# Hymba layer: the MLP's two products computed with seven of eight block products, up before down

## The chip, the cores and the metric

The kernel runs on one core of one Trainium2 chip. The metric is the device time of one execution in microseconds. Beside the runs without a profile there is one profiled execution, from which all views of the profile come.

## The reference

One decoder layer on x (1 x 1024 x 1024, float32): an attention part with two groups of heads, then the MLP that the change is about, then a last norm. Token count T = 1024, model width D = 1024, hidden width FF = 4096.

```python
def rmsnorm(x, g):
    xf = x.astype(jnp.float32)
    y = xf * lax.rsqrt(jnp.mean(jnp.square(xf), axis=-1, keepdims=True) + NORM_EPS)
    return (y * g.astype(jnp.float32)).astype(x.dtype)
...
    h = h + mix @ w_o
    v = rmsnorm(h, mlp_norm_g)
    h = h + jnp.square(jax.nn.relu(v @ w_up)) @ w_down
return rmsnorm(h, final_norm_g)
```

## The kernel before

Every float32 product is made of three TensorE products. A value is split into a high part (a cast to fp32r) and a low part (the value minus the high part), and a matmul group sums high x high, high x low and low x high. The high parts are casts on ScalarE or VectorE, the low parts subtractions on VectorE or POOL.

After attention `wo_ml(t)` (L1022) finishes the residual h for 128 tokens at a time, stores it to DRAM (`h_dram`) and normalises it; `v_tr(t)` (L1036) transposes the result on TensorE (8 transposes, L1042) into `vT`, the moving operand of the up product. The MLP runs in 16 chunks of 256 hidden columns. For each chunk:

- `w_split` (L1049) loads raw weights and splits them: high part on VectorE (L1053), low part on POOL (L1054).
- `up` makes four PSUM groups of 24 matmuls (L1076; 128x128 weights, 512 tokens). `up_act` squares the relu: ScalarE reads the bank (L1083), VectorE squares (L1084), ScalarE casts (L1085), POOL makes the low part (L1086).
- `down` (L1119) makes sixteen groups of 6 matmuls (L1131), and VectorE adds each to the residual in SBUF, `hacc` (L1133).

The order of TensorE is the order of the code (a manual schedule); a scheduler orders the other engines and SP's DMA queue. The main loop (end of the function) alternates: up of chunk c + 1, then down of chunk c; the last two chunks' down products are done together, 12 matmuls a group, and `finish_half` (L1137) norms and stores each 128 tokens behind them. `hacc` is loaded from `h_dram` (L1156) while the first chunk's up product runs. Half of that first product (th = 0) is placed between the last transposes. TensorE's MLP work is 16 x 96 up matmuls and 16 x 96 down matmuls.

Of the kernel before, what the change touches and what calls it, by code (L numbers as in the profile page):

```python
# [23 lines left out]
def tile_hymba_block(  # L24
# [1032 lines left out]
    def w_up_chunk(c):
        return [w_split(w_up[u * 512:(u + 1) * 512, c * FC * P:(c + 1) * FC * P].rearrange("(k p) f -> p k f", p=P),
                        [4, FC * P], s8) for u in range(2)]

    def w_down_chunk(c):
        return [w_split(w_down[(c * FC + u) * P:(c * FC + u + 1) * P, :], [D], wd_tile) for u in range(FC)]

    for t in range(NT):
        wo_ml(t)
        if t >= 2:
            v_tr(t - 2)
        if t == NT - 3:
            wu0 = w_up_chunk(0)
    def up_mm(wu, u, th):  # L1070
        tsl = slice(th * 512, (th + 1) * 512)
        ps = up_ps.tile([P, 512], F32, name="up", tag="up")
        n = 0
        for k in range(ND):
            for a, b in ((0, 0), (0, 1), (1, 0)):
                nc.tensor.matmul(ps[:], wu[k // 4][:, a, k % 4, u * P:(u + 1) * P], vT[:, b, k, tsl],  # L1076
                                 start=(n == 0), stop=(n == 3 * ND - 1))
                n += 1
        return ps

    def up_act(ps, hl, th, r):
        tsl = slice(th * 512, (th + 1) * 512)
        nc.scalar.activation(r[:], ps[:], AF.Relu)  # L1083
        nc.vector.tensor_mul(r[:], r[:], r[:])  # L1084
        nc.scalar.copy(hl[:, 0, tsl], r[:])  # L1085
        nc.gpsimd.tensor_sub(hl[:, 1, tsl], r[:], f(hl[:, 0, tsl]))  # L1086

    def up(c, wu):
        hid = []
        for u in range(FC):  # L1090
            hid.append(s8([P, 2, T]))
        for th in range(2):
            for u in range(FC):
                up_act(up_mm(wu, u, th), hid[u], th, relu_tile())
        return hid

    h0 = [s8([P, 2, T]) for _ in range(FC)]
    for u in range(FC):
        up_act(up_mm(wu0, u, 0), h0[u], 0,
               hp_pool.tile([P, D], F32, name="junk", tag="junk", bufs=3)[:, :512])  # L1100
        v_tr(NT - 2 + u)
# [4 lines left out]
    dn_ps = ctx.enter_context(tc.tile_pool(name="dn_ps", bufs=5, space=PSUM, reuse_waits="tile"))  # L1106
    mp_pool = ctx.enter_context(tc.tile_pool(name="mp_pool", bufs=1, reuse_waits="tile"))
    hacc = mp_pool.tile([P, NT, D], F32, name="hacc")
    gfb = mp_pool.tile([P, D], F32, name="gfb")
    def wd_tile(shape):  # L1110
        return mp_pool.tile(shape, F32R, name="wd", tag="wd", bufs=4)

    def relu_tile():
        return mp_pool.tile([P, 512], F32, name="rl", tag="rl", bufs=2)

    for u in range(FC):
        up_act(up_mm(wu0, u, 1), h0[u], 1, relu_tile())

    def down(cs, hid):  # L1119
        wd = [w for c in cs for w in w_down_chunk(c)]  # L1120
        nk = len(wd)
        final = cs[-1] == NCH - 1
        for t in range(NT):
            tsl = slice(t * P, (t + 1) * P)
# [85 lines left out]
```

## Time and profile before

| | |
|---|---|
| median of 3 runs | 1288.97 us (1288.13 to 1289.02) |
| profiled execution, span | 1286.3 us |
| PE (TensorE) busy | 1232.0 us, 96% |
| DVE (VectorE) busy | 721.8 us, 56% |
| POOL (GpSimd) busy | 480.7 us, 37% |
| ACT (ScalarE) busy | 401.1 us, 31% |
| read from HBM, written | 75.53 MB, 23.07 MB |

The profiled execution's own time stands here as its span: 2.7 us below the median of the other runs. Busy shares are averages over the whole span; the chain of waits and the timelines show which engine is waited for in a stage. Times in views are counted from the span's start.

### The profile page before, as it was taken

How to read it: one execution, taken by the hardware profiler on the slowest of the kernel's cores; microseconds unless marked ns; L12 is line 12 of the kernel's file. 1: busy time of each engine (PE TensorE's matmuls, PEld its weight loads, DVE VectorE, ACT ScalarE, POOL GpSimd, SP SyncE). 2: the span in 40 equal slices, each digit the busy share in tenths (PEclk: the TensorE clock that was granted, in tenths of full speed). 3: DMA queues.
4: the chain of work that ended last, by engine and by line, in shares of the span. 5: the costliest groups of instructions: out<-in, count | busy, mean ns of one | idle time of the engine just before them, and what ended most of it. 6: DMA issues, size and time to landing. Idle time of an engine off the chain costs nothing.

```text
span 1286.3 us, 15538 instructions
## 1 busy us (share of the span) xinstructions
PE 1232.0 (96%) x5808; PEld 1006.7 (78%) x5808; DVE 721.8 (56%) x1120; ACT 401.1 (31%) x916; POOL 480.7 (37%) x445
## 2 busy tenths in 40 slices
PE   9998988888799999999999999999999999999997
PEld 8877766666578888888888888888888888888886
DVE  8685589999997854564433443344334334433424
ACT  6433466666667831232011001101100110011022
POOL 3433444555634532216434224323432342243221
PEclk9999999999999999999999999999999999999999
DMA  6416635244511244644211112101201121021002
GB/s 214 123 58 204 157 74 123 58 103 105 186 58 50 88 160 146 222 156 162 72 59 56 43 33 66 49 33 50 66 34 47 52 61 38 33 67 49 1 33 98
DMA packets 64874, 112.17 MB, mean 87 GB/s; under 512 B 6304, under 2 KB 40608, under 8 KB 64288
## 3 DMA queue, kind: packets, MB, share of 16 engines
q1 hardware_dynamic: 64800, 111.20, 28.2%
q8 instruction: 45, 0.74, 0.2%
q14 instruction: 29, 0.24, 0.1%
HBM read 75.53 MB, written 23.07 MB: 77 GB/s over the span
## 4 chain that ended last, share of the span: by engine, by line
PE 69%; DVE 4%; ACT 1%; issue 1%; DMA 1%; POOL 0%; DVEq 0%; POOLq 0%; ACTq 0%; SPq 0%
PE dn L1131 28%; PE up L1076 27%; PE wo_p L962 3%; PE s L962 3%; DVE w L536 2%; PE mtr L828 1%; DMA kl<-klo 1%; PE s L740 1%; PE s L742 1%; PE s L741 1%; PE mav L845 1%; PE mav L846 1%; PE mav L847 1%; PE s L743 1%; PE s L744 1%
## 5 line engine op out<-in xcount | busy, mean ns | idle before, releaser
L1131 PE MATMUL dn<-wd,s 128*128 128x512 f32 x1536 | 360.7, 395 | 0.0
L1076 PE MATMUL up<-vT,s 128*128 128x512 f32 x1536 | 351.8, 389 | 0.6 <-DVE vT L693 0.4
L1131 PEld LDWEIGHTS dn<-wd,s 128*128 128x128 f32 x1536 | 288.3, 188 | 69.8
L1076 PEld LDWEIGHTS up<-vT,s 128*128 128x128 f32 x1536 | 288.1, 188 | 61.2 <-DVE vT L693 0.7
L1133 DVE TENSOR_TENSOR hacc<-hacc,dn 128x512 f32<-128x512 f32 x240 | 165.0, 688 | 147.1 <-PE dn L1131 147.0
L1054 POOL TENSOR_TENSOR wd<-raw,wd 128x1024 fp32r<-128x1024 f32 x32 | 82.1, 2565 | 321.8 <-DVE wd L1053 321.2
L1083 ACT ACTIVATE rl<-up 128x512 f32<-128x512 f32 x62 | 37.2, 599 | 516.5 <-PE up L1076 507.7
L1084 DVE TENSOR_TENSOR rl<-rl 128x512 f32<-128x512 f32 x62 | 47.8, 770 | 166.9 <-ACT rl L1083 166.9
L1086 POOL TENSOR_TENSOR s<-rl,s 128x512 fp32r<-128x512 f32 x62 | 80.7, 1302 | 87.7 <-ACT s L1085 87.7
L488 PE MATMUL mm<-xh,wt 128*128 128x512 f32 x256 | 87.9, 395 | 0.0
L549 PE MATMUL tr<-zid,b 128*128 128x128 f32 x288 | 52.6, 290 | 35.1 <-DVE al L557 25.5
L1054 POOL TENSOR_TENSOR s<-raw,s 128x1024 fp32r<-128x1024 f32 x32 | 77.6, 2427 | 21.6 <-DVE s L1053 12.8
L542 POOL TENSOR_TENSOR b<-b,w 128x512 f32<-128x512 f32 (+2 forms) x57 | 59.5, 1043 | 58.8 <-DVE w L536 39.5
L549 PEld LDWEIGHTS tr<-zid,b 128*128 128x128 f32 x288 | 33.0, 142 | 58.4 <-DVE al L557 44.2
L1053 DVE CAST wd<-raw 128x1024 fp32r<-128x1024 f32 x32 | 27.9, 872 | 76.2 <-DMA raw<-in_w_down_dram 76.1
L536 DVE TENSOR_TENSOR_SCAN w<-w,zid 128x129 f32<-128x129 f32 (+1 forms) x64 | 64.3, 1007 | 1.8 <-ACT w L531 1.6
L263 PE MATMUL acc<-wt,xh 128*128 128x448 f32 (+1 forms) x256 | 62.6, 378 | 1.4 <-ACT xh L214 1.4
L1085 ACT CAST s<-rl 128x512 fp32r<-128x512 f32 x62 | 38.6, 622 | 60.8 <-DVE rl L1084 60.8
L263 PEld LDWEIGHTS acc<-wt,xh 128*128 128x128 f32 x256 | 47.7, 188 | 8.9 <-ACT xh L214 2.0
L488 PEld LDWEIGHTS mm<-xh,wt 128*128 128x128 f32 x256 | 48.2, 189 | 8.3 <-issue 0.2
L488 PE MATMUL mm<-xl,wt 128*128 128x512 f32 x128 | 52.6, 411 | 0.0
L557 DVE TENSOR_TENSOR al<-tr,ah 128x512 fp32r<-128x512 f32 (+2 forms) x80 | 47.8, 597 | 5.8 <-ACT ah L556 5.4
(287 smaller groups left out, 1823.4 us busy)
## 6 DMA issues: line engine op xcount, KB each, us to landing
raw<-in_w_up_dram SPq DMA_DIRECT2D x32, 512.0 KB, 3.8
raw<-in_w_down_dram SPq DMA_DIRECT2D x32, 512.0 KB, 3.5
wr<-in_w_in_dram SPq DMA_DIRECT2D x24, 256.0 KB, 2.9
raw<-in_w_o_dram SPq DMA_DIRECT2D x8, 512.0 KB, 3.5
ht<-h_dram SPq DMA_DIRECT2D x8, 512.0 KB, 4.3
h_dram<-ht SPq DMA_DIRECT2D x8, 512.0 KB, 2.8
hacc<-h_dram SPq DMA_DIRECT2D x8, 512.0 KB, 7.6
xr<-in_xT_dram SPq DMA_DIRECT2D x14, 256.0 KB, 5.2
```

The lines of the kernel that those rows point to most:

```text
L263: nc.tensor.matmul(accs[t][:, :width], a[:, kk, t * P:(t + 1) * P], wts[kk][:, b, :width], start=(kk == 0 and p == 0), stop=done)
L488: nc.tensor.matmul(ps[:], wt[:, a, k % 4, :], b[:, k, tsl], start=(n == 0), stop=(n == 3 * ND - 1))
L536: nc.vector.tensor_tensor_scan(rv, rv, inject, init, ALU.mult, ALU.add)
L542: eng.tensor_mul(b[:, :n], b[:, :n], w[:, 1:n + 1])
L549: nc.tensor.transpose(tr[:, j * P:(j + 1) * P], sb_a[h, Q, C, j][:, s * P:(s + 1) * P], identf[:])
L557: nc.vector.tensor_sub(al[:, lo:], tr[:, lo:], f(ah[:, lo:]))
L962: nc.tensor.matmul(ps, hl[e][:, a, tsl], wt[e][:, b, dh * 512:(dh + 1) * 512], start=(n == 0), stop=(n == 11))
L1054: nc.gpsimd.tensor_sub(wt[:, 1], wr[:], f(wt[:, 0]))
L1076: nc.tensor.matmul(ps[:], wu[k // 4][:, a, k % 4, u * P:(u + 1) * P], vT[:, b, k, tsl], start=(n == 0), stop=(n == 3 * ND - 1))
L1086: nc.gpsimd.tensor_sub(hl[:, 1, tsl], r[:], f(hl[:, 0, tsl]))
L1131: nc.tensor.matmul(ps[:], hid[u][:, a, tsl], wd[u][:, b, dsl], start=(n == 0), stop=(n == 3 * nk - 1))
L1133: nc.vector.tensor_add(hacc[:, t, dsl], hacc[:, t, dsl], ps[:])
```

## The change

The up product hid = v x w_up is written as 2x2 blocks: per "quad" of 256 hidden columns the weights are four blocks A (each 512 of D by 128 columns), the transposed v four blocks B (512 of D by 512 tokens). Four blocks of the result come from seven block products in place of eight (the Winograd form): three use plain blocks of the weights, four use sums of blocks. A block product is 12 matmuls (`prod`).

- B11 and B21 are split straight out of the transposes of the first four token blocks, and their raw values go through DRAM (`r_dram`); R12 and R22 keep the raw values of the last four. The setup loop (`for j in range(4)`) makes the sums T1 to T4 and B22 out of them, each with its high and low part: per turn 5 casts on ScalarE, 6 operations on VectorE, 3 on POOL.
- For the first four quads, products 1 and 2 (which need B11 and B21 alone) are done ahead: `pre_quad(0)` and `(1)` between the last transposes, `(2)` and `(3)` behind the setup loop.
- `quad_w` makes the weight sums (4 VectorE operations) and splits seven weight blocks, low parts on POOL. `step` runs a product and adds on VectorE out of PSUM; `relu2` squares the relu. The sums of hidden values that down needs (s1 to s4) are made on VectorE, and all hidden values and sums go to DRAM: seven stores of 256 KB per quad.
- Down has the same form: seven chunks of 512 hidden columns, 7 products of 24 matmuls each, that collect in seven accumulators, four of which start from the residual (16 loads of 256 KB). Hidden values are loaded back (`ar`, 512 KB per product) and split: cast on ScalarE, low part on POOL. The last 512 hidden columns (two quads) are done plainly: 192 matmuls, 12 a group, with `finish_half` behind each.
- All of up is done before down begins. PSUM pools are renamed (3 + 5 banks for up, 8 for down); `raw_pool` has 2 buffers in place of 3.

The diff, cut to its core:

```diff
+    def split2(hi, lo, src, eng):
+        nc.scalar.copy(hi, src)
+        eng.tensor_sub(lo, src, f(hi))
+
+    def prod(ps, w, bv, start, stop):
+        n, last = 0, 3 * HD - 1
+        for k in range(HD):
+            for a, b in ((0, 0), (0, 1), (1, 0)):
+                nc.tensor.matmul(ps, w[:, a, k, :], bv[:, b, k, :], start=start and n == 0, stop=n == last,
+                                 skip_group_check=True)
+                n += 1
...
+    def pre_quad(q):
+        x = x_of[q]
+        ps = a_ps.tile([P, 512], F32, name="pa", tag="pa")
+        prod(ps[:], x[:, 0], B11, True, True)
+        p1 = o_tile("p1")
+        nc.scalar.copy(p1[:], ps[:])
+        prod(ps[:], x[:, 1], B21, False, True)
+        hid = o_tile("ho")
+        nc.scalar.activation(hid[:], ps[:], AF.Relu)
+        nc.vector.tensor_mul(hid[:], hid[:], hid[:])
+        p1_of[q] = (p1, hid)
+        store_hid(q, V_A11, hid[:])
...
+    pre_quad(0)
+    v_tr(NT - 2)
+    pre_quad(1)
+    pre_w(3)
+    v_tr(NT - 1)
...
+    nc.sync.dma_start(f(T1[:, 1]), r_dram[0][:])
+    nc.sync.dma_start(f(T4[:, 1]), r_dram[1][:])
+    for j in range(4):
+        c = slice(j * P, (j + 1) * P)
+        tt = s8([P, 4, HD, P], F32)
+        nc.vector.tensor_sub(tt[:, 0], R12[:, :, c], f(T1[:, 1, :, c]))
+        nc.vector.tensor_sub(tt[:, 1], R22[:, :, c], tt[:, 0])
+        nc.gpsimd.tensor_sub(tt[:, 2], R22[:, :, c], R12[:, :, c])
+        nc.vector.tensor_sub(tt[:, 3], f(T4[:, 1, :, c]), tt[:, 1])
+        for n_, (bv, sv) in enumerate(((T2, tt[:, 1]), (T1, tt[:, 0]), (T3, tt[:, 2]), (B22, R22[:, :, c]), (T4, tt[:, 3]))):
+            split2(bv[:, 0, :, c], bv[:, 1, :, c], sv, nc.gpsimd if n_ in (2, 3) else nc.vector)
...
+    pre_quad(2)
+    pre_quad(3)
...
+        split2(a22[:, 0], a22[:, 1], r22, nc.gpsimd)
+        w[V_A22] = a22[:]
+        nc.vector.tensor_add(r22, r21, r22)
+        nc.vector.tensor_sub(r21, r11, r21)
+        nc.vector.tensor_sub(r11, r22, r11)
+        nc.vector.tensor_sub(r12, r12, r11)
...
+        for tl, v, key, r_ in ((y, 0, V_S2, r11), (y, 1, V_S1, r22), (z, 0, V_S3, r21), (z, 1, V_S4, r12)):
+            split2(tl[:, v, 0], tl[:, v, 1], r_, nc.gpsimd)
...
+            elif what == 2:
+                prod(s_["a"][:], w[V_A12], B21, False, True)
+                s_["c11"] = o2_tile("ho")
+                nc.scalar.activation(s_["c11"][:], s_["a"][:], AF.Relu)
+                nc.gpsimd.tensor_mul(s_["c11"][:], s_["c11"][:], s_["c11"][:])
+                store_hid(q, V_A11, s_["c11"][:])
+            elif what == 6:
+                prod(bank("b"), w[V_S2], T2, True, True)
+                s_["u2"] = o_tile("u2")
+                nc.vector.tensor_add(s_["u2"][:], s_["b"][:], s_["p1"][:])
...
+        order = (1, 2, 6, 5, 7, 3, 4) if pair else (6, 5, 7, 3, 4) if pre else (1, 6, 5, 7, 2, 3, 4)
...
+    for q in range(NQ - 2):
+        quads([q], q < NPRE)
+    quads([NQ - 2, NQ - 1])
...
+    nc.sync.dma_start(gfb[:], gfin.to_broadcast([P, D]))
+    for q in range(4):
+        nc.sync.dma_start(acc[2][:, q], h_dram[q][:, 0:512])
+        nc.sync.dma_start(acc[3][:, q], h_dram[q][:, 512:])
+        nc.sync.dma_start(acc[4][:, q], h_dram[q + 4][:, 0:512])
+        nc.sync.dma_start(acc[7][:, q], h_dram[q + 4][:, 512:])
...
+        for i in (1, 2, 3, 5, 7, 6, 4):
+            ar = dn_pool.tile([P, 2, 512], F32, name="ar", tag="ar", bufs=4)
+            nc.sync.dma_start(ar[:], hv_dram[c][:, A_OF[i]])
+            av = s8([P, 2, 2, 512])
+            split2(av[:, 0], av[:, 1], ar[:], nc.gpsimd)
+            prep(i)
+            for q in range(4):
                 ps = dn_ps.tile([P, 512], F32, name="dn", tag="dn")
                 n = 0
-                for u in range(nk):
+                for u in range(2):
                     for a, b in ((0, 0), (0, 1), (1, 0)):
...
+                dst = acc[i][:, q]
+                if c == 0 and i in (1, 5, 6):
+                    nc.scalar.copy(dst, ps[:])
+                else:
+                    nc.vector.tensor_add(dst, dst, ps[:])
...
+    for u in range(4):
+        split2(lh[u][:, 0], lh[u][:, 1], hr[:, u], nc.gpsimd)
+        lb.append(s8([P, 2, D]))
+        split2(lb[u][:, 0], lb[u][:, 1], lw[:, u], nc.vector)
+    for q in range(4):
+        g = {i: acc[i][:, q] for i in acc}
+        nc.vector.tensor_add(g[2], g[2], g[1])
+        nc.vector.tensor_add(g[6], g[6], g[1])
+        nc.vector.tensor_add(g[5], g[5], g[6])
+        nc.vector.tensor_add(g[3], g[3], g[5])
+        nc.gpsimd.tensor_add(g[4], g[4], g[6])
+        nc.gpsimd.tensor_add(g[4], g[4], g[7])
+        nc.vector.tensor_add(g[7], g[7], g[5])
```

Three places of the order. First, VectorE where the MLP begins. Before (junk and rl are hidden values, s and wd split weights, vT the low parts of the transposes):

```order
L1033 SCALAR_TENSOR_TENSOR junk<-ht,nss,ssq_s 128x1024
L693 TENSOR_TENSOR vT<-vtr,vT 128x4x128
L1084 TENSOR_TENSOR junk<-junk 128x512
L693 TENSOR_TENSOR vT<-vtr,vT 128x4x128 x2
L1084 TENSOR_TENSOR junk<-junk 128x512
L693 TENSOR_TENSOR vT<-vtr,vT 128x4x128 x2
L1053 CAST s_6402<-raw 128x1024
L1053 CAST s_6407<-raw 128x1024
L1053 CAST wd<-raw 128x1024
L1084 TENSOR_TENSOR rl<-rl 128x512 x3
```

Now (ho are hidden values, r are R12 and R22, t the T tiles, s the loop's scratch tiles; L1076 are the low parts of `split2`):

```order
L1122 TENSOR_TENSOR ho<-ho 128x512 x2
L1151 TENSOR_TENSOR s_6389<-r_5836,t_6383 128x512
L1151 TENSOR_TENSOR s_6404<-r_5836,t_6383 128x512
L1152 TENSOR_TENSOR s_6389<-r_5837,s_6389 128x512
L1076 TENSOR_TENSOR t_6383<-s_6389,t_6383 128x4x128
L1152 TENSOR_TENSOR s_6404<-r_5837,s_6404 128x512
L1076 TENSOR_TENSOR t_6382<-s_6389,t_6382 128x4x128
L1076 TENSOR_TENSOR t_6383<-s_6404,t_6383 128x4x128
L1154 TENSOR_TENSOR s_6389<-t_6386,s_6389 128x512
L1154 TENSOR_TENSOR s_6404<-t_6386,s_6404 128x512
L1076 TENSOR_TENSOR t_6382<-s_6404,t_6382 128x4x128
```

The two squares of early hidden values stand ahead of the setup loop, and in place of a few splits VectorE has the loop's 24 operations, of which the first ten are shown; two more squares and the weight sums of the first quad follow them.

Second, SP's queue where the residual is loaded. Before, among the first up products (h_dram holds the residual):

```order
L1031 DMA h_dram_109<-ht 128x1024
L1031 DMA h_dram_110<-ht 128x1024
L1156 DMA hacc<-h_dram_103 128x1024
L1156 DMA hacc<-h_dram_104 128x1024
...
L1156 DMA hacc<-h_dram_110 128x1024
L1157 DMA gfb<-in_gfin_dram 128x1024
L1051 DMA raw<-in_w_down_dram 128x1024
L1051 DMA raw<-in_w_up_dram 128x4x256 x2
L1051 DMA raw<-in_w_down_dram 128x1024 x2
L1051 DMA raw<-in_w_up_dram 128x4x256 x2
```

Now, between up and down (the acc tiles are the accumulators, wr the weights of down, ar its hidden values):

```order
L1108 DMA hl_dram<-ho 128x512 x7
L1285 DMA gfb<-in_gfin_dram 128x1024
L1108 DMA hl_dram<-ho 128x512
L1287 DMA acc_8697<-h_dram_103 128x512
L1288 DMA acc_8698<-h_dram_103 128x512
L1289 DMA acc_8702<-h_dram_107 128x512
L1290 DMA acc_8700<-h_dram_107 128x512
...
L1290 DMA acc_8700<-h_dram_110 128x512
L1299 DMA wr<-in_w_down_dram 128x2x1024 x2
L1331 DMA ar<-hv_dram_5840 128x1024 x7
L1299 DMA wr<-in_w_down_dram 128x2x1024 x2
```

The loads of the residual have moved behind the last hidden store of up, and the first weights and hidden values of down stand behind them.

Third, POOL ahead of the last stage. Before (s are the hidden values' low parts, fss the sums of `finish_half`):

```order
L1054 TENSOR_TENSOR s_10187<-raw,s_10187 128x1024
L1086 TENSOR_TENSOR s_9921<-rl,s_9921 128x512
L1054 TENSOR_TENSOR wd<-raw,wd 128x1024 x2
L1086 TENSOR_TENSOR s_10190<-rl,s_10190 128x512
L1086 TENSOR_TENSOR s_10191<-rl,s_10191 128x512
L1086 TENSOR_TENSOR s_10190<-rl,s_10190 128x512
L1086 TENSOR_TENSOR s_10191<-rl,s_10191 128x512
L1143 TENSOR_TENSOR fss<-fss 128x1
L82 TENSOR_SCALAR rs_mean<-fss 128x1
L83 TENSOR_TENSOR fss<-rs_mean,mhalf 128x1
```

Now (acc_8702 is accumulator 4, lh the split hidden values of the last two quads; L1372 and L1373 are the loop's two POOL sums):

```order
L1076 TENSOR_TENSOR s_10705<-ar,s_10705 128x1024
L1076 TENSOR_TENSOR s_10709<-wr,s_10709 128x1024
L1372 TENSOR_TENSOR acc_8702<-acc_8702,acc_8701 128x512
L1373 TENSOR_TENSOR acc_8702<-acc_8702,acc_8700 128x512
L1372 TENSOR_TENSOR acc_8702<-acc_8702,acc_8701 128x512
L1373 TENSOR_TENSOR acc_8702<-acc_8702,acc_8700 128x512
L1076 TENSOR_TENSOR lh_10748<-hr,lh_10748 128x1024
L1076 TENSOR_TENSOR lh_10749<-hr,lh_10749 128x1024
L1076 TENSOR_TENSOR lh_10752<-hr,lh_10752 128x1024
L1076 TENSOR_TENSOR lh_10753<-hr,lh_10753 128x1024
L1372 TENSOR_TENSOR acc_8702<-acc_8702,acc_8701 128x512
L1373 TENSOR_TENSOR acc_8702<-acc_8702,acc_8700 128x512
L1372 TENSOR_TENSOR acc_8702<-acc_8702,acc_8701 128x512
```

The four low parts of the plain rest stand behind four sums of accumulator 4, where before the low parts of the last chunk were the only work.

## Rows read from the trace of the kernel before

**Rows 1.** the page's head and its first part: busy time, share of the span, instructions

```profile
span 1286.3 us, 15538 instructions
...
PE 1232.0 (96%) x5808; PEld 1006.7 (78%) x5808; DVE 721.8 (56%) x1120; ACT 401.1 (31%) x916; POOL 480.7 (37%) x445
```

**Rows 2.** the page's chain that ended last, by line: shares of the span

```profile
PE dn L1131 28%; PE up L1076 27%; PE wo_p L962 3%; PE s L962 3%; DVE w L536 2%; PE mtr L828 1%; DMA kl<-klo 1%; PE s L740 1%; PE s L742 1%; PE s L741 1%; PE mav L845 1%; PE mav L846 1%; PE mav L847 1%; PE s L743 1%; PE s L744 1%
```

**Rows 3.** the chain in order of time, MLP: start us, length us, engine and line

```profile
569.38 5.49 PE up L1076 x24
574.87 0.87 PE vtr L1042 x8
...
638.33 21.77 PE up L1076 x96
660.11 22.39 PE dn L1131 x96
...
1234.27 44.81 PE dn L1131 x192
```

**Rows 4.** groups of equal shape on VectorE, ScalarE, POOL: busy us, mean ns | idle before

```profile
L1133 DVE TENSOR_TENSOR hacc<-hacc,dn 128x512 f32<-128x512 f32 x240 | 165.0, 688 | 147.1 <-PE dn L1131 147.0
...
L1030 DVE SCALAR_TENSOR_TENSOR ht<-wo_p,rs_mla,ht 128x512 f32<-128x512 f32 x16 | 11.7, 744 | 5.1 <-PE wo_p L962 5.1
...
L1033 DVE SCALAR_TENSOR_TENSOR junk<-ht,nss,ssq_s 128x1024 f32<-128x1024 f32 x8 | 10.3, 1284 | 7.6 <-POOL nss L83 7.6
...
L1085 ACT CAST s<-rl 128x512 fp32r<-128x512 f32 x62 | 38.6, 622 | 60.8 <-DVE rl L1084 60.8
...
L1017 ACT ACTIVATE junk<-ht 128x1024 f32<-128x1024 f32 x8 | 8.5, 1062 | 10.6 <-DVE ht L1030 10.6
...
L1086 POOL TENSOR_TENSOR s<-rl,s 128x512 fp32r<-128x512 f32 x62 | 80.7, 1302 | 87.7 <-ACT s L1085 87.7
L1054 POOL TENSOR_TENSOR s<-raw,s 128x1024 fp32r<-128x1024 f32 x32 | 77.6, 2427 | 21.6 <-DVE s L1053 12.8 <-POOL s L1086 8.8
```

**Rows 5.** timeline of TensorE, 581 to 584 us: start, length, instructions, [idle before]

```profile
582.38 0.49 PE L1076 MATMUL up<-vT,s 128*128 128x512 f32 x1 [0.29 <-ACT vT L692]
583.23 0.96 PE L1076 MATMUL up<-vT,s 128*128 128x512 f32 x3 [0.36 <-DVE vT L693]
```

**Rows 6.** timelines of VectorE and of POOL, 583 to 602 us

```profile
585.79 2.89 DVE L1053 CAST wd<-raw 128x1024 fp32r<-128x1024 f32 x1
589.41 2.07 DVE L1084 TENSOR_TENSOR rl<-rl 128x512 f32<-128x512 f32 x1 [0.73 <-ACT rl L1083]
...
600.35 0.69 DVE L1084 TENSOR_TENSOR rl<-rl 128x512 f32<-128x512 f32 x1 [4.80 <-ACT rl L1083]
...
585.40 5.54 POOL L1054 TENSOR_TENSOR s<-raw,s 128x1024 fp32r<-128x1024 f32 x2 [0.68 <-DVE s L1053]
...
601.78 1.29 POOL L1086 TENSOR_TENSOR s<-rl,s 128x512 fp32r<-128x512 f32 x1 [4.20 <-ACT s L1085]
```

**Rows 7.** windows (busy us of five engines, PEclk, DMA share, GB/s), and a DMA issue

```profile
10.00:15.00 5.00, 5.00 (x27) 4.63 (x26) 5.00 (x9) 4.65 (x8) 1.04 (x1) 1.00 0.98 355
...
580.00:585.00 5.00, 4.35 (x23) 3.26 (x22) 3.12 (x4) 2.08 (x4) 1.31 (x1) 1.00 1.03 418
...
raw<-in_w_down_dram SPq DMA_DIRECT2D x32, 512.0 KB, 3.5
```

**Rows 8.** two windows at half the clock, and an instruction just before the first

```profile
98.69 0.55 PE L392 MATMUL tr<-zid,ce 128*128 128x128 f32 x3 [3.10 <-DVE rstd_b L453]
...
99.70:103.00 3.30, 3.30 (x14) 2.70 (x12) 1.50 (x2) 1.06 (x2) 0.00 (x0) 0.50 0.61 225
...
311.40:314.60 3.20, 3.20 (x14) 2.94 (x13) 3.20 (x7) 2.96 (x8) 2.79 (x3) 0.50 0.76 168
```

**Rows 9.** timelines of VectorE and of POOL, 616 to 623 us

```profile
618.38 1.27 DVE L1133 TENSOR_TENSOR hacc<-hacc,dn 128x512 f32<-128x512 f32 x2
...
617.87 1.74 POOL L1086 TENSOR_TENSOR s<-rl,s 128x512 fp32r<-128x512 f32 x1
```

More of the change, by code (lines that the diff above doesn't have):

```diff
@@ L1057, in w_up_chunk @@
[L1057 to L1062, printed above, removed]
+            if t < 4:
+                bb = (B11, B21)[dq]
+                split_out(tr[:], bb[:, 0, :, c], bb[:, 1, :, c])
+                stg = vraw_pool.tile([P, HD, P], F32, name="stg", tag="stg", bufs=3)
+                nc.scalar.copy(stg[:], tr[:])
+                nc.sync.dma_start(r_dram[dq][:, :, c], stg[:])
+            else:
+                nc.scalar.copy((R12, R22)[dq][:, :, c], tr[:])
@@ L1068, in tile_hymba_block @@
         if t == NT - 3:
[L1069 to L1101, printed above, removed]
+            for q in range(3):
+                pre_w(q)
+    pre_quad(0)
[3 more added lines that the diff above has]
+    v_tr(NT - 1)
     wo_stack.close()
@@ L1105, in tile_hymba_block @@
     rope_stack.close()
[L1106 to L1124, printed above, removed]
-            for dh in range(2):
-                dsl = halves[dh]
+    bcd_ps = mlp_psum.enter_context(tc.tile_pool(name="bcd_ps", bufs=5, space=PSUM, reuse_waits="tile"))
+    vb_stack = ExitStack()
+    vb_pool = vb_stack.enter_context(tc.tile_pool(name="vb_pool", bufs=1, reuse_waits="tile"))
@@ L1134, in down @@
-                if final:
-                    finish_half(t, dh)
-    def finish_half(t, dh):
+                dst = acc[i][:, q]
+                if c == 0 and i in (1, 5, 6):
+                    nc.scalar.copy(dst, ps[:])
+                else:
+                    nc.vector.tensor_add(dst, dst, ps[:])
+    for c in range(NQ // 2 - 1):
+        down(c)
+    dn_stack.close()
+    ld_pool = ctx.enter_context(tc.tile_pool(name="ld_pool", bufs=1, reuse_waits="tile"))
+    lh = [ld_pool.tile([P, 2, T], F32R, name=f"lh{u}") for u in range(2)]
@@ L1138, in finish_half @@
+    for q in range(4):
+        g = {i: acc[i][:, q] for i in acc}
[6 more added lines that the diff above has]
+        nc.vector.tensor_add(g[7], g[7], g[5])
+    fin = {}
+    def finish_half(t, dh, hx):
         if dh == 0:
-            fin.append((mp_pool.tile([P, 4], F32, name="fss", tag="fss", bufs=3), s8([P, D], F32)))
```

222 lines of the change are left out of this document (191 added, 31 removed).

## The prediction

> **What bounds the kernel now.** I read the head of the page first: TensorE is busy for 1232.0 of the 1286.3 us [rows 1]. Then the chain by line: the down and up products hold 28% and 27% of the span [rows 2]. The chain in order of time shows how: from 569.38 it is product after product, 96 up matmuls in 21.77 us and 96 down matmuls in 22.39, with one hand-over between [rows 3]. So the MLP is TensorE's own time, and other engines count only where TensorE is made to wait. One up matmul costs 21.77 / 96 = 0.2268 us, one down matmul 0.2332. The MLP's whole matmul time is 16 x 21.77 + 14 x 22.39 + 44.81 = 706.6 us.
>
> The profiled execution lasts 1286.3 us, 2.7 below the median of the runs shown (1288.97). The sum is made against 1286.3, and 2.7 is added at the end. A difference under 0.2%, 2.6 us, can't be told from none.
>
> **What goes.** Up now has 16 quads x 7 products x 12 = 1344 matmuls, down 7 chunks x 7 x 24 + 192 = 1368, so 360 of 3072 are gone. The shape stays (a 128x128 weight tile, 512 columns), so I take each product's own row: 1344 x 0.2268 + 1368 x 0.2332 = 304.8 + 319.0 = 623.8, **82.8 us less**. If the new tiles of up run at down's 0.2332 it is 74.2; if down runs at up's rate it is 91.5.
>
> **What comes, 1: the start of up.** TensorE is at 569.38 when its up products begin, in both kernels. Ahead of the first product that needs T2 stand four early pairs of products (96 x 0.2268 = 21.8) and two blocks of transposes (2 x 0.87 [rows 3]). The second product of a pair adds to the bank from which ScalarE copies the first, so it waits for a copy (0.62 by a cast of the same size [rows 4]) and a hand-over (about 0.36 [rows 5]): 1.0 each. The last transposes so end at 569.4 + 11.0 + 1.7 + 2.0 = 584.1. Then R12 and R22 are copied out (0.6 each, to 585.3) and the setup loop makes T1 to T4 and B22: 24 VectorE operations, each with both inputs in SBUF, and 12 on POOL. Such an operation takes 0.69 on VectorE (600.35, with POOL idle until 601.78 [rows 6]) and 1.30 on POOL [rows 4].
>
> Do the two run side by side? In rows 6, VectorE's operation at 589.41 took 2.07 us in place of 0.69 and ended just after the POOL pair that ran from 585.40; the cast at 585.79 took 2.89, and that POOL pair 5.54 in place of 2 x 2.4. An operation that meets the other engine's waits for it. I take them one after the other: 24 x 0.69 + 12 x 1.30 = 32.2, so 617.5. Behind them VectorE has two squares and three weight combinations for S2 (3.5), then come ScalarE's cast (0.62) and a low part on POOL (1.30): T2 and S2 are there at 622.9. TensorE has work for 23.5 of the 53.5 us from 569.4, so it idles 30, against 1 us in the same place before (0.29 + 0.36 and their hand-overs [rows 5]): **+29**. If the loop's two engines overlapped in full, VectorE's 16.6 us alone would set it, the product would start near 607.3, and the term is +13; if eight hand-overs of 0.36 between the engines are added it is +32. The Trainium skill (SBUF — State Buffer, "Who interferes with whom") says that a VectorE instruction with two SBUF inputs and a GpSimd instruction that reads SBUF share a port pair, and the later one blocks fully. By that rule the term is +29, by engines that run freely +13; rows 6 side with the rule.
>
> **2: between up and down.** Before, up and down products alternated, and the residual was loaded under running products. Now down can't start until all of up is through, and SP issues in order: the last hidden store, 16 loads of 256 KB into the accumulators, the first 2 MB of down weights, then the first 512 KB of hidden values. Let up's last matmul end at U. The last store waits for an addition and a square (0.69 + 0.74 [rows 4], with hand-overs U + 1.75). Behind it 4.2 MB go at 355 to 418 GB/s [rows 7], say 11 us, the weights take 5.0 and the values 1.25 at 418. A single 512 KB load lands 3.5 us after its issue [rows 7], 2.2 more than its bytes need: U + 21.2. ScalarE's cast (1.06) and POOL's low part (2.43) follow [rows 4]: U + 24.7. Nothing of TensorE's lies in between: **+25**, between +21 (no latency, all at 418) and +29 (all at 355, the latency once for the weights and once for the values). The same chain stands before the second and third products of the first chunk, whose low parts come from the same POOL: **+2.5** (0 to 5).
>
> **3: the last 512 rows.** POOL's order is two pairs of accumulator sums, then the four low parts of the last hidden rows. The sums wait for the last Strassen product's evictions. Let that product end at E. Its first group is evicted at about E - 3.5; four sums of 1.30 bring POOL to E + 1.7, and four low parts of 2.43 to E + 11.4. The first output group needs all four: its last three matmuls (0.7) end at E + 12.1 in place of E + 2.8, so 9.3 us are lost, and VectorE's 1024-wide low parts (1.28 [rows 4]) push between POOL's. I take **+12**, between +8 (sums that start earlier) and +17 (POOL waits for each of VectorE's four).
>
> **4: the clock.** Twice in the kernel before, TensorE got a granted clock of 0.50, the level of 1.2 GHz: the first time just after it had been idle for 3.10 us; the windows at 0.50 are 3.30 and 3.20 us long, full of work [rows 8]. That costs 1.7 us each time. The changed kernel has three idle stretches longer than 3.10: **+5** (0 to 9).
>
> **5: work that should be hidden.** In up each full quad has 7 low parts and one square on POOL (8 x 1.30 = 10.4), and on VectorE 11 operations with both inputs in SBUF (8 x 0.69 + 3 x 0.74 = 7.7) and 5 additions from PSUM (3.4). TensorE takes 84 x 0.2268 = 19.05 per quad. 10.4 + 7.7 = 18.1 fits. The additions from PSUM do not wait for POOL: at 618.38 two took 1.27 together beside POOL's operations, as long as two alone [rows 9]. An early quad has 13.6 us of TensorE time against 5 x 1.30 + 7.7 = 14.2, a loss of 0.6 four times. In down each chunk has 10 POOL low parts (24.3), and 8 VectorE operations 1024 wide (10.2) beside 28 additions from PSUM (19.3); TensorE takes 39.2, so 34.5 of exclusive work fits with little to spare. On SP a quad's seven stores of 256 KB, each waiting for its square or sum, stand ahead of later quads' weight loads; a quad later is 19 us, so this costs nothing unless VectorE falls a quad behind. I take **+4** for both stages (0 to 45, the second rival).
>
> Sum: -82.8 + 29 + 25 + 2.5 + 12 + 5 + 4 = -5.3. Span 1281.0, and with 2.7 a time of **1283.7 us**. The seven-product saving is nearly eaten by two places at which TensorE stands still.
>
> **The rivals.**
> *The setup runs side by side (faster).* The term of 29 becomes 13: 1283.7 - 16 = 1267.7. For it: POOL's twelve operations are 15.6 us in all, and those that fall where VectorE waits for one of ScalarE's 20 casts cost nothing. Against it: rows 6.
> *Blocking reaches the additions from PSUM (slower).* Then POOL's 10.4 and all of VectorE's 11.1 add up to 21.5 per full quad against 19.05, and 6.5 + 11.1 = 17.6 against 13.6 per early one: 12 x 2.4 + 4 x 4.0 = 45 in place of the 4 above, a time near 1325. It decides as soon as the two together exceed 19.05 per quad. For it: VectorE works its queue in order, so an addition stands behind a blocked operation, and TensorE waits for a bank. Against it: rows 9, and five banks that give slack.
> *The new tiles take the slow rate.* Up at 0.2332 gives 1344 x 0.0064 = 8.6 back: 1292.3. For it: two rates in one kernel for the same shape show that the operands, or where they lie, matter; against it: the shapes and the weights' side are those of up.
> *Every wait at its upper end.* +32, +29, +5, +17, +9 in place of 29, 25, 2.5, 12, 5 is 18.5 more: 1302.
> That the change doesn't remove the matmuls is excluded: they are counted in TensorE's order, 1344 and 1368.
>
> **How the numbers follow.** Forecast 0.32, its own range 1276 to 1291; setup side by side 0.22; slow rate 0.19; all waits long 0.15; blocking 0.12. The forecast lies under the bound of 1286.4 for four fifths of its chance and within 0.2% for the rest; the slow rate is half within, half above 1291.5. Faster 0.26 + 0.22 = 0.48; same 0.06 + 0.09 = 0.15; slower 0.10 + 0.15 + 0.12 = 0.37. The range runs from 1265, a little under the fast rival, to 1308, over the long waits, and leaves out the blocking rival and little else.
>
> **What would show it.** In the changed profile: 2712 MLP matmuls at 0.227 and 0.233; one idle stretch of TensorE of about 25 us that ends on POOL's or VectorE's last setup operation near 622; one of about 25 us before the first down product, which ends on POOL's low part behind the accumulator loads; one of 9 to 12 us before the last 192 matmuls; between these no TensorE idle time over 2 us per quad or chunk. The prediction is wrong if setup operations show 0.69 beside POOL's, if the boundary is under 15 us, or if TensorE waits inside the quads.

## The result and the profile after

The changed kernel takes 1297.2 us (median of 4 runs, 1295.69 to 1300.3) against 1288.96 before: 1.0062 times as long, 95% interval 1.0045 to 1.0079. It is slower by 0.6%. The sum said 5.3 us less; it is about 8 us more. The profiled execution's span is 1293.9 us, 7.6 over that of before.

The page of the changed kernel, its head, busy times and chain:

```profile
span 1293.9 us, 15840 instructions
...
PE 1167.7 (90%) x5448; PEld 946.9 (73%) x5448; DVE 946.3 (73%) x1300; ACT 531.2 (41%) x1078; POOL 643.9 (50%) x539
...
PE 24%; DVE 8%; POOL 7%; DMA 4%; issue 3%; ACT 1%; SPq 0%; DVEq 0%; POOLq 0%; ACTq 0%
```

TensorE did get 360 instructions less (5448 in place of 5808) and 64 us less busy time than in [rows 1]. But the chain that was nearly all TensorE in the MLP [rows 2, 3] now runs through VectorE, POOL and transfers as well. Where TensorE stands still is in its timeline; the main ones after an idle time of over half a microsecond are these, and the first two matmuls of the last stage (start, length, instructions, [idle before and releaser]):

```profile
572.03 3.02 PE L1082 MATMUL pa<-b,s 128*128 128x512 f32 x12 [0.68 <-ACT p L1118]
...
587.11 5.73 PE L1082 MATMUL pa<-b,s 128*128 128x512 f32 x24 [1.11 <-ACT p L1118]
599.12 5.30 PE L1082 MATMUL pa<-b,s 128*128 128x512 f32 x12 [6.28 <-ACT p L1118]
617.47 4.99 PE L1082 MATMUL pb<-t,s 128*128 128x512 f32 x12 [13.05 <-ACT s L1075]
672.27 4.59 PE L1082 MATMUL pd<-b,s 128*128 128x512 f32 x12 [1.92 <-DVE u L1223]
...
791.56 3.05 PE L1082 MATMUL pd<-b,s 128*128 128x512 f32 x12 [0.72 <-DVE u L1223]
...
812.08 3.06 PE L1082 MATMUL pd<-b,s 128*128 128x512 f32 x12 [0.78 <-DVE u L1223]
...
890.59 7.54 PE L1082 MATMUL pa<-b,s 128*128 128x512 f32 x24 [4.56 <-ACT p L1209]
950.92 0.80 PE L1340 MATMUL dn<-s,s 128*128 128x512 f32 x1 [24.79 <-ACT s L1075]
953.49 19.21 PE L1340 MATMUL dn<-s,s 128*128 128x512 f32 x72 [1.77 <-DVE s L1076]
...
1224.32 0.63 PE L1400 MATMUL dn<-s,lh 128*128 128x512 f32 x2
1234.44 1.65 PE L1400 MATMUL dn<-s,lh 128*128 128x512 f32 x3 [9.50 <-POOL lh L1076]
1237.20 1.65 PE L1400 MATMUL dn<-s,lh 128*128 128x512 f32 x3 [1.11 <-POOL lh L1076]
```

The three forecast stalls are there: at 599 and 617 (the setup), at 950.92 (between up and down), at 1234 (the last 512 rows). The fourth was not forecast at this size: in up TensorE waits once in the early quads (672.27), then from 791.56 on once in each quad, for VectorE's additions, and 4.56 us for ScalarE in the last two (890.59). Up's last matmul ends at 926.1 (950.92 less 24.79).

What products cost can be read from the chain in order of time (start, length, what):

```profile
688.00 2.80 PE pc L1082 x12
690.80 2.73 PE pa L1082 x12
...
973.51 206.01 PE dn L1340 x908
```

Products that move B11 or B21 (pa) take 2.73 / 12 = 0.2275 us a matmul, the other five of seven 0.233, down's 0.2269. All of it: 16 x (2 x 2.73 + 5 x 2.80) = 311.4, 1176 x 0.2269 = 266.8 and 192 at the 0.2332 of before (44.8) make 623.0, which is 83.6 us less than before. So the saving came as forecast (82.8), and what is wrong lies in what was added.

| stage of the changed kernel | forecast | found | how it is found |
|---|---|---|---|
| matmuls | -82.8 | -83.6 | above |
| start of up, to 622.3 | +29, clock 1.7 | +26.5 | 53.9 from 568.35, less 26.4 of work, less 1 before |
| quads, 622.3 to 926.1 | +4 | +17.1 | 303.8, less 15 early products' worth |
| boundary, to 973.5 | +27.5, clock 1.7 | +30.8 | 47.4 less 73 x 0.2269 |
| last stage, from 1224.3 | +12, clock 1.7 | +17.5 | 62.3 (to 1286.6, TensorE's end) less 44.8 |

The row of the quads is worked out so: 19 products of the early quads at 2.80 (one was already done at 622.3) and 12 full quads of 2 x 2.73 + 5 x 2.80 = 19.46 are 286.7 us of work. The five rows sum to 8.3; up's first product started 0.8 us earlier than before (568.35 against 569.14), so this agrees with the 7.6 of the spans.

The starts of the products say where in up the 17.1 us lie. From 622.3 to the first full quad at 679.5 it is 4.0, the wait at 672.27 and half clock behind it. The next five quads, to 776.8, lose nothing. The five from there to 880.2 lose 6.1, and the last two 7.1, of which 4.56 are the wait at 890.59.

**The quads.** One turn of a full quad, from one weight load to the next, put together from the timelines of POOL, SP, ScalarE and VectorE in order of time:

```profile
749.00 4.24 POOL L1076 TENSOR_TENSOR s<-s,s 128x512 fp32r<-128x512 f32 x3 [1.89 <-ACT s L1075]
...
753.27 0.94 SPq L1170 DMA_DIRECT2D s<-in_w_up_dram  x2
...
757.46 0.62 ACT L1075 CAST s<-s 128x512 fp32r<-128x512 f32 x1 [7.50 <-DMA s<-in_w_up_dram]
...
758.16 2.66 POOL L1076 TENSOR_TENSOR s<-s,s 128x512 fp32r<-128x512 f32 x2 [4.92 <-ACT s L1075]
...
759.35 0.59 ACT L1213 ACTIVATE ho<-pa 128x512 f32<-128x512 f32 x1
...
760.78 1.04 POOL L1214 TENSOR_TENSOR ho<-ho 128x512 f32<-128x512 f32 x1
761.78 1.30 POOL L1076 TENSOR_TENSOR a<-s,a 128x512 fp32r<-128x512 f32 x1
...
761.86 1.77 DVE L1242 TENSOR_TENSOR s<-ho 128x512 f32<-128x512 f32 x1 [4.99 <-POOL ho L1214]
...
766.56 1.77 DVE L1256 TENSOR_TENSOR s<-ho,s 128x512 f32<-128x512 f32 x1
...
769.66 4.26 POOL L1076 TENSOR_TENSOR s<-s,s 128x512 fp32r<-128x512 f32 x3 [1.88 <-ACT s L1075]
...
773.95 0.94 SPq L1170 DMA_DIRECT2D s<-in_w_up_dram  x2
```

Read it as a ring. The load of the next quad's weights (753.27) is issued when POOL has made the last low parts out of the weights before (749.00 + 4.24). It lands 4 us later; ScalarE casts A11 and A12, and only behind these comes its relu of c11 (759.35), though TensorE had finished that product at 751.9. POOL's square (L1214) stands behind POOL's two low parts. VectorE, in order, waits 4.99 us for that square, and behind s3 (L1242) stand the next quad's weight sums, their casts, POOL's low parts, and the next load at 773.95. The ring takes 20.7 us, TensorE's work 19.46. No other engine is full; the ring is longer than TensorE's work. TensorE doesn't show it at once: in this turn it still runs without a gap, on operands that were made ahead, and only from 791.56 on, when this lead is used up, does it wait.

Blocking is part of the ring's length. VectorE's operations at 761.86 and 766.56, both with both inputs in SBUF, took 1.77 us each in place of 0.69, each beside a low part of POOL: about 2.2 of the 20.7 us. No run takes this away by itself.

### The profile page after: what moved, and what is told of

It reads as the page before. It is cut to its first block, busy times and chain, and to the rows that moved or that the text cites. A ratio compares the mean times of both kernels' runs of the same rounds, so it can differ in the third digit from the quotient of the medians.

```text
span 1293.9 us, 15840 instructions
## 1 busy us (share of the span) xinstructions
PE 1167.7 (90%) x5448; PEld 946.9 (73%) x5448; DVE 946.3 (73%) x1300; ACT 531.2 (41%) x1078; POOL 643.9 (50%) x539
## 5 line engine op out<-in xcount | busy, mean ns | idle before, releaser
L1340 PE MATMUL dn<-s,s 128*128 128x512 f32 x1176 | 270.6, 392 | 27.7 <-ACT s L1075 24.8
L1340 PEld LDWEIGHTS dn<-s,s 128*128 128x128 f32 x1176 | 222.5, 189 | 75.9 <-ACT s L1075 25.2
L1076 POOL TENSOR_TENSOR s<-s,s 128x512 fp32r<-128x512 f32 x88 | 123.3, 1418 | 121.3 <-ACT s L1075 120.8
L1076 POOL TENSOR_TENSOR s<-ar,s 128x1024 fp32r<-128x1024 f32 x49 | 130.8, 2673 | 52.3 <-ACT s L1075 52.3
L1346 DVE TENSOR_TENSOR acc<-acc,dn 128x512 f32<-128x512 f32 x184 | 118.2, 678 | 24.7 <-PE dn L1340 24.5
L1075 ACT CAST s<-s 128x512 fp32r<-128x512 f32 x88 | 51.5, 619 | 195.8 <-DMA s<-in_w_up_dram 86.1
L1082 PE MATMUL pa<-b,s 128*128 128x512 f32 x384 | 97.7, 406 | 13.4 <-ACT p L1118 8.7
L1082 PEld LDWEIGHTS pa<-b,s 128*128 128x128 f32 x384 | 74.0, 195 | 32.8 <-ACT p L1118 10.4
L1076 DVE TENSOR_TENSOR s<-wr,s 128x1024 fp32r<-128x1024 f32 x28 | 53.7, 1918 | 27.9 <-ACT s L1075 27.9
L1076 POOL TENSOR_TENSOR s<-wr,s 128x1024 fp32r<-128x1024 f32 x21 | 52.5, 2502 | 32.7 <-ACT s L1075 32.7
L1400 PE MATMUL dn<-s,lh 128*128 128x512 f32 x192 | 49.4, 420 | 12.8 <-POOL lh L1076 12.8
```

Source lines behind the costliest of these rows:

```text
L1075: nc.scalar.copy(hi, src)
L1076: eng.tensor_sub(lo, src, f(hi))
L1082: nc.tensor.matmul(ps, w[:, a, k, :], bv[:, b, k, :], start=start and n == 0, stop=n == last, skip_group_check=True)
L1340: nc.tensor.matmul(ps[:], av[:, a, u, q * P:(q + 1) * P], bv[i][:, b, u], start=(n == 0), stop=(n == 5))
L1346: nc.vector.tensor_add(dst, dst, ps[:])
L1400: nc.tensor.matmul(ps[:], lh[u][:, a, tsl], lb[u][:, b, halves[dh]], start=(n == 0), stop=(n == 11))
```

## The experiments

Each was run against the kernel before on its own chip, so the ratios to before are compared: the changed kernel's is 1.0062. Inside one run, stages are compared by the distances between its own rows, since the part ahead of the MLP, which no edit touches, differs between runs: TensorE's first product that waits starts at 570.67 in one and at 575.03 in another.

### The square of c11 on VectorE

```diff
-                nc.gpsimd.tensor_mul(s_["c11"][:], s_["c11"][:], s_["c11"][:])
+                nc.vector.tensor_mul(s_["c11"][:], s_["c11"][:], s_["c11"][:])
```

> The square of c11 moves from POOL to VectorE, nothing else. Theory: in the changed kernel up runs on a ring of 20.5 us per full quad, longer than TensorE's 19.4 (weight load, POOL's low parts of A11 and A12, the c11 square behind them, VectorE's s3 that waits for it, the weight sums behind s3, POOL's low parts, next load). Without POOL's square in it the ring is about 1.5 to 2.5 us shorter: the twelve full quads take about 236 us in place of 246.6, the time falls by 8 to 10 us to about 1288. Rival: the summed work of VectorE and POOL sets the pace, and moving 1.0 us from one to the other changes it by less than 2 us.

Measured: 1305.92 us, ratio 1.0131 (1.0116 to 1.0146). Slower, against the forecast of the theory and beyond the rival's bound too. Its rows, of VectorE and of TensorE:

```profile
762.62 1.39 DVE L1214 TENSOR_TENSOR ho<-ho 128x512 f32<-128x512 f32 x1 [7.76 <-ACT ho L1213]
...
753.23 3.05 PE L1082 MATMUL pd<-b,s 128*128 128x512 f32 x12 [1.42 <-DVE u L1223]
774.52 3.06 PE L1082 MATMUL pd<-b,s 128*128 128x512 f32 x12 [1.46 <-DVE u L1223]
```

The period is 21.2 us. VectorE's square waits 7.76 us for ScalarE's relu, and in the new order c12's addition and square stand behind it where they had been done during the wait. The ring is there, but I had cut it in the wrong place: the link that ties c11 to the weight load is first of all ScalarE's order; POOL's stood less than 1 us behind it (relu done at 759.94, square begun at 760.78 in the changed kernel). Nearly the same summed work with a longer period speaks against the rival.

### c11 wholly on VectorE

```diff
-                nc.scalar.activation(s_["c11"][:], s_["a"][:], AF.Relu)
-                nc.gpsimd.tensor_mul(s_["c11"][:], s_["c11"][:], s_["c11"][:])
+                nc.vector.tensor_scalar(s_["c11"][:], s_["a"][:], 0.0, None, ALU.max)
+                nc.vector.tensor_mul(s_["c11"][:], s_["c11"][:], s_["c11"][:])
```

> c11 is made on VectorE alone, the relu out of PSUM and the square, so neither ScalarE's relu (queued behind the casts of A11 and A12, which wait for the next weight load) nor POOL's square stands between it and VectorE's s3. Theory of the ring, as the run with the square alone on VectorE (period 21.2 us) leaves it: the wait for the weight load goes out of VectorE's queue, the period falls to TensorE's own 19.4 us per full quad, the twelve quads take 233 to 238 us, time 8 to 12 us less than the changed kernel's 1297. Rival, summed work: VectorE gets 0.7 to 1.4 us more per quad, the period stays at 20.5 us or grows.

Measured: 1287.9 us, ratio 0.9989 (0.9979 to 0.9999), 9 us less than the changed kernel. Up to 776.8 both kernels have TensorE's own period, so the place to compare is behind it. The first products of two late quads, in TensorE's timeline of this run:

```profile
854.73 2.90 PE L1082 MATMUL pa<-b,s 128*128 128x512 f32 x12
...
874.18 5.62 PE L1082 MATMUL pa<-b,s 128*128 128x512 f32 x24
```

The same two in the changed kernel:

```profile
859.67 2.90 PE L1082 MATMUL pa<-b,s 128*128 128x512 f32 x12
...
880.15 5.88 PE L1082 MATMUL pa<-b,s 128*128 128x512 f32 x24
```

The period is 19.45, TensorE's own, in place of 20.48, and TensorE shows no idle time in any of the ten quads from 679.66 to 874.18. The wait of 4.56 us in the last two quads is down to 0.28 and 1.48. VectorE has more work than before the edit, and is held off by POOL no less (its operations at 757.91, 759.61 and 763.72 took 1.78 us each). So the order of waits set the pace of up's full quads, not the amount of work. That a further buffer for the weights would open the ring as well was not tried.

### The first weights of down ahead of most residual loads

```diff
+            if c == 0 and i == 2:
+                acc_loads()
...
-    for q in range(4):
-        nc.sync.dma_start(acc[2][:, q], h_dram[q][:, 0:512])
```

> SP issues the first weights and hidden values of down ahead of 13 of the 16 residual loads. Theory: the queue's order makes the boundary; TensorE's wait before the first down product falls from 24.8 to about 14 us, time 9 to 11 us less. Rival: the same bytes are needed by the first four products anyway, TensorE waits for accumulators or for POOL a product later: less than 3 us gained.

Measured: ratio 1.0024 (1.0013 to 1.0035), about 5 us less than the changed kernel. TensorE's timeline:

```profile
947.33 0.79 PE L1341 MATMUL dn<-s,s 128*128 128x512 f32 x1 [16.83 <-ACT s L1075]
949.90 13.33 PE L1341 MATMUL dn<-s,s 128*128 128x512 f32 x48 [1.78 <-DVE s L1076]
964.95 5.74 PE L1341 MATMUL dn<-s,s 128*128 128x512 f32 x24 [1.72 <-POOL s L1076]
```

The first wait falls by 8.0 us to 16.83, and later waits grow by about 2. Between the two forecasts: order matters, but 2.5 MB of weights and values still stand in the stall.

### The first weights and values under the last products

The pool of down's weights and values is opened where B11 and B21 lay, as soon as the last two quads are through products 1 and 2:

```diff
             for q in qs:
                 step(what, q)
+            if pair and what == 2:
+                va_stack.close()
+                first_loads()
```

> The first weights and hidden values of down get the place of B11 and B21, free once products 1 and 2 of the last two quads are through, and are loaded there under the other ten products; the residual loads stay behind the last hidden store. Theory: the 24.8 us wait at the boundary is transfers in a row that need not stand there; TensorE's wait there falls to under 5 us, some microseconds return where VectorE waits for the residual, time 15 to 22 us less than 1297. Rival: the residual loads (11 us) hold the second product's additions, or splits on POOL are late: 8 us or less.

Measured: 1276.35 us, ratio 0.9892 (0.9877 to 0.9907), 21 us less than the changed kernel and faster than the one before. TensorE's timeline at the boundary:

```profile
931.29 1.56 PE L1357 MATMUL dn<-s,s 128*128 128x512 f32 x6
937.13 23.13 PE L1357 MATMUL dn<-s,s 128*128 128x512 f32 x91 [4.28 <-DVE ho L1250]
```

Of 24.8 us 4.28 are left, and that wait is for VectorE to empty the last bank of up. The residual loads, still behind the last store, cost TensorE nothing: VectorE waits for them, up to 2.36 us at 953.72, and TensorE's matmuls run on. That eight banks cover the delay is argued, not shown.

### Accumulator 4's sums on VectorE

```diff
-        nc.gpsimd.tensor_add(g[4], g[4], g[6])
-        nc.gpsimd.tensor_add(g[4], g[4], g[7])
+        nc.vector.tensor_add(g[4], g[4], g[6])
+        nc.vector.tensor_add(g[4], g[4], g[7])
```

> The eight sums of accumulator 4 before the last stage move from POOL to VectorE. Theory: the four low parts of the last hidden rows wait on POOL only because these sums stand ahead of them; without them TensorE's wait before the last 192 matmuls (9.5 and three times 1.1 us, with the half clock 17 us) falls to under 5 us, time 8 to 13 us less. Rival: VectorE, with eight more operations, is late next: less than 3 us gained.

Measured: ratio 1.0016 (1.0006 to 1.0025), about 6 us less. In the changed kernel POOL's timeline reads:

```profile
1223.72 1.30 POOL L1372 TENSOR_TENSOR acc<-acc,acc 128x512 f32<-128x512 f32 x1 [12.60 <-DVE acc L1346]
...
1231.60 11.07 POOL L1076 TENSOR_TENSOR lh<-hr,lh 128x1024 fp32r<-128x1024 f32 x4
```

POOL was idle for 12.6 us ahead of the sums, as they waited for evictions, and the low parts came 8 us after that. With the sums away TensorE's timeline is:

```profile
1230.47 1.16 PE L1400 MATMUL dn<-s,lh 128*128 128x512 f32 x3 [2.34 <-DVE s L1076]
1233.77 1.65 PE L1400 MATMUL dn<-s,lh 128*128 128x512 f32 x3 [2.15 <-DVE s L1076]
1237.07 43.91 PE L1400 MATMUL dn<-s,lh 128*128 128x512 f32 x182 [1.66 <-DVE s L1076]
```

The idle time falls from 12.8 to 6.2 us, and its releaser is now VectorE's own low parts, which were beside POOL's: the rival took half of the gain.

### The setup's POOL operations on VectorE

```diff
-        nc.gpsimd.tensor_sub(tt[:, 2], R22[:, :, c], R12[:, :, c])
+        nc.vector.tensor_sub(tt[:, 2], R22[:, :, c], R12[:, :, c])
...
-            split2(bv[:, 0, :, c], bv[:, 1, :, c], sv, nc.gpsimd if n_ in (2, 3) else nc.vector)
+            split2(bv[:, 0, :, c], bv[:, 1, :, c], sv, nc.vector)
```

> The setup loop's twelve POOL operations move to VectorE, which then has 36. If VectorE's and POOL's operations exclude each other, the sum falls from 24 x 0.69 + 12 x 1.30 = 32.2 to 24.8 us and the first product that needs T2 starts up to 5 us earlier than the 617.5 of the changed kernel: 2 to 5 us less in all. If they run side by side, VectorE's chain gets 12 x 0.69 = 8.3 us longer: 5 to 8 us more.

Measured: ratio 1.0049 (1.0034 to 1.0064), which can't be told from the changed kernel's by the time alone. The stage can be told: from the first product that waits (572.03 in the changed kernel, 573.41 here) to the first that needs T2 (617.47; 614.12 here) it is 45.4 us in one and 40.7 in the other. Twelve operations more on VectorE, and it is ready 4.7 us earlier. That is what the first forecast said, but the run doesn't show that exclusion alone did it. The changed kernel's rows have two causes (timelines of ScalarE, VectorE and POOL, with VectorE busy without a gap from 593.98 to 611.16):

```profile
592.80 2.69 ACT L1075 CAST t<-s 128x512 fp32r<-128x512 f32 x5 [5.75 <-POOL s L1153]
...
593.98 1.80 DVE L1076 TENSOR_TENSOR t<-s,t 128x512 fp32r<-128x512 f32 x1 [7.33 <-ACT t L1075]
...
602.18 10.10 POOL L1076 TENSOR_TENSOR t<-s,t 128x512 fp32r<-128x512 f32 x1 [3.60 <-ACT t L1075]
612.24 1.25 POOL L1076 TENSOR_TENSOR a<-s,a 128x512 fp32r<-128x512 f32 x1
```

One cause is order: ScalarE's next cast waited for a subtraction of POOL, VectorE for that cast, and so VectorE stood still for 7.33 us. With POOL's operations on VectorE that wait is gone. The other is exclusion: VectorE's operation at 593.98 took 1.80 us in place of 0.69 beside POOL's, and one POOL operation of 1.3 us lasted 10.10 and ended 1.1 us after VectorE's run of operations did. The Trainium skill (SBUF — State Buffer, "Who interferes with whom") says that whichever of the two issues first holds the shared ports for its whole instruction and the other blocks fully. The rows agree that the other blocks; that POOL stays blocked over a run of VectorE's instructions is what the 10.10 us show beyond that.

### The setup in the order of need

T2 and the first quad's weight sums first, then T1, T3, B22 and T4; all on VectorE; the early products' copies ahead of the casts on ScalarE:

```diff
+    pre_quad(2)
+    pre_quad(3)
...
+    t_split(T2, [tt[:, 1] for tt in tts], nc.vector)
+    w_first = quad_w(0, True)
+    t_split(T1, [tt[:, 0] for tt in tts], nc.vector)
```

> The setup makes T2 and the first quad's weight sums first, all of it on VectorE, with the early products' copies ahead of it on ScalarE. Theory: the first product that needs T2 starts after 2 squares, 8 sums, 8 low parts and the first weight sum or so, 20 operations of 0.69 from 585, at 600 to 603 in place of 617.5, so 12 to 15 us less. Rival: ScalarE's casts or a later product's operand (T3, B22, T4) end the wait instead, under 6 us gained.

Measured: ratio 1.0042 (1.0027 to 1.0057): nothing that can be told from the changed kernel. The product with T2 did start early (606.19; 32.9 us after the first wait in place of 45.4). But then, in TensorE's timeline and in the window of the early quads (busy us of PE, PEld, DVE, ACT, POOL):

```profile
637.18 4.31 PE L1082 MATMUL pd<-b,s 128*128 128x512 f32 x12 [3.33 <-DVE u L1234]
...
606.00:680.00 74.00, 66.28 (x257) 51.61 (x258) 65.61 (x78) 19.56 (x35) 41.65 (x28) 0.92 0.44 149
```

VectorE is busy for 65.6 of 74 us. It has the rest of the setup and four quads' sums to do whenever TensorE starts. From the first T2 product to the first full quad it is 70.1 us (606.19 to 676.25) in place of 62.0 (617.47 to 679.48): 8 of the 12.5 us came back inside the early quads, and 1 more behind them.

### All of it

The edits of c11, of the first weights and of the setup, and at the last stage the hidden values loaded ahead of the last chunk's, with accumulator 4's and 7's sums behind the first output groups:

```diff
             finish_half(t, dh, hx)
+        if t < 4:
+            g = {i: acc[i][:, t] for i in acc}
+            nc.vector.tensor_add(g[4], g[4], g[6])
+            nc.vector.tensor_add(g[4], g[4], g[7])
+            nc.vector.tensor_add(g[7], g[7], g[5])
```

> The three edits together, and at the last stage the low parts of the last hidden rows ahead of accumulator 4's sums, which go to VectorE behind the first output groups, with their load ahead of the last chunk's. If the stalls are separate, they add up: 10 + 18 + 12 + 12 less than 1297, near 1245, with TensorE idle under 12 us from 569 on. If one stall only hands its time to the next, 1270 or more.

Measured: 1246.87 us, ratio 0.9666 (0.9651 to 0.968). TensorE's timeline from 880 on has three waits over 1.5 us:

```profile
883.38 3.06 PE L1082 MATMUL pa<-b,s 128*128 128x512 f32 x12 [1.51 <-ACT p L1220]
920.14 250.72 PE L1371 MATMUL dn<-s,s 128*128 128x512 f32 x1098 [4.31 <-DVE ho L1261]
...
1192.92 43.51 PE L1430 MATMUL dn<-s,lh 128*128 128x512 f32 x182 [2.56 <-DVE s L1076]
```

The stalls of the boundary, the quads and the last stage are separate and add up: 9 us for c11 and 22 for the first weights from their own runs, 13 in the last stage (here 48.8 us from 1187.65 to TensorE's end, in place of 62.3), and the 5 that the next run finds for the setup make 49, against 51 together. TensorE's idle times in the MLP, those at the start and in the early quads among them, still sum to about 28 us, more than the 12 I expected.

### All of it, with the old setup

The run above without its setup edit.

> The run with all edits, but with the setup of the changed kernel. If the 12 us that the new setup gains before the first T2 product are handed back in the early quads, because VectorE has the same operations to do by then (about 85% busy there), the time is that of the run with all edits, 1247, within 3 us. If the gain counts, the time is 8 to 12 us more.

Measured: 1250.73 us, ratio 0.9707 (0.9689 to 0.9725), 0.4% or 5 us more than with the new setup. That is neither of the two forecasts: of the 12.5 us gained before the first T2 product about 5 count, and the rest is handed back.

### Squares of c22, c12 and c21 on ScalarE

```diff
-        nc.vector.scalar_tensor_tensor(dst, src, 0.0, src, ALU.max, ALU.mult)
+        nc.scalar.activation(dst, src, AF.Relu)
+        nc.scalar.activation(dst, dst, AF.Square)
```

> The run with all edits, and up's squares of c22, c12 and c21 as two ScalarE operations each (relu, square) in place of one on VectorE. If VectorE's work bounds the early quads (four quads of 17 operations beside the setup), they gain 1 to 2 us each, 4 to 8 us in all, about 1241. If the order of ScalarE's queue matters more (casts of weights wait behind squares), the time stays or grows by up to 10 us.

Measured: 1244.57 us, ratio 0.9663 (0.9646 to 0.968). That is the ratio of the run with all edits. In TensorE's timeline the waits of the early quads shrink (3.46 and 1.92 become one of 1.47), and the wait ahead of the last two quads grows from 1.5 to 4.91. Less work on VectorE helps where VectorE is full. That the order of ScalarE's queue takes it back fits the releaser of the 4.91, ScalarE's copy, but no run shows it by itself.

## Why the prediction was wrong

**The matmuls: right.** 83.6 us saved against 82.8. The new tiles took the slow rate (the third rival's point, 5 of 7 products), and down took the fast one (0.2269 in place of 0.2332); that the two cancel is luck.

**Start of up: near in size, the mechanism right in part.** 26.5 us with its clock, against 29 and 1.7. The engines did exclude each other (1.80 us on VectorE, 10.10 on POOL). But the operations did not stand one after the other for 32.2 us from 585.3: VectorE was through with them and two squares at 611.16, and for 7.33 us of that time it waited, by way of ScalarE's queue, for a POOL subtraction. The first T2 product came at 617.47, not 622.9. I had also missed that ScalarE's copies for the early products stand behind its casts (6.28 us of the idle time); the run with the setup on VectorE has 0.94 there, and the next wait grows from 13.05 to 15.94.

**Boundary: right.** 24.79 us of waiting against 25, then 1.77 and 0.81 against 2.5. The run with the early loads shows the cause.

**Last stage: right mechanism, too small.** 12.8 us of idle time against 12, and over 4 more at half the clock: from 1234 to 1243, across the three waits of 1.1 us, the granted clock was 0.50.

**The clock: undersized.** I counted three stretches at half the clock; there were six (after 599, 617, 672, 890, 951 and 1234).

**The quads: the step that failed.** Step 5 said that "10.4 + 7.7 = 18.1 fits" and that stores ahead of a weight load cost "nothing unless VectorE falls a quad behind", and gave up and down 4 us together. Down cost none: from 973.51 its matmuls run without a gap worth a microsecond until the last chunk. Up's quads cost 17.1, and one of the prediction's own signs of being wrong is there: TensorE waits inside the quads. The step summed work per engine and compared it with TensorE's; it never followed one quad's weights through load, cast, low part, sum, cast, low part and back to the load, with what stands ahead of each in its queue. That ring is 20.7 us long, and 13 of the 17.1 us lie in the full quads, behind the point at which TensorE's lead is used up; 4 lie in the early quads, where step 5 had 2.4. The two runs on c11 show the ring: moving the square alone made it 21.2, freeing it from ScalarE's queue made it TensorE's own 19.45, though VectorE had an operation more both times.

With the quads at the measured value in place of 4 the sum of the forecast is +7.8, against +7.6 in the trace and +8 in the medians. That it fits so well is luck in part: with the clock shared out as in the table, the start of up came out 4 us under its forecast, the boundary and the last stage 5 over.

The second rival named the right stage with the wrong mechanism. Additions from PSUM did not wait for POOL (one at 630.86 took 0.69 us beside POOL's low parts of 627.09 to 631.66); operations with both inputs in SBUF did, which makes the ring longer, and the order of the queues closed it. The time lay inside the range, but on the other side of the kernel before.

## What to carry to other kernels

Summing each engine's work per turn tells only whether a stage can keep up, not whether it does: follow one turn's data around until it frees the buffer of the next load, count what stands ahead of each step in its in-order queue, and compare that length with the bound. Look for it late in the stage: here five quads passed before the bound engine waited at all. When a change turns an alternation into two phases, price what had been hidden under the other phase, and look for a buffer that comes free early enough to load the second phase's first operands. And before a stall is removed, ask which engine is nearly full just behind it: most of the setup's gain was handed back within four quads.
